# One decoder layer in single precision: squares of the head norms on ScalarE, and the pieces of h built in single steps

## The chip, the cores and the metric

One Trainium2 chip, one core of it. The time is the device time of one execution in microseconds; a kernel is given by the median of several runs. Inside the core TensorE (PE) does matrix products, with its weight loads beside them; VectorE (DVE), ScalarE (ACT) and GpSimd (POOL) do everything elementwise; SyncE and the queues of ACT start transfers between HBM and the on-chip memory. Each engine takes its own instructions in a fixed order and stands still when the next one has to wait.

## What is computed

```python
def decoder_layer(x, ...):                       # x: 1024 prompt rows and 8 x 4 sample rows, 1024 wide
    h = rmsnorm(x, ln1)
    proj = h @ w_in
    aq, ak, av, sh, sB, sC, dqkv, dz, da, db, gl = jnp.split(proj, split_at, axis=-1)
    oa = attn_fn(aq, ak, av, sinks)              # A) banded attention with sinks
    ob = sB * causal_dwconv(sC * sh)             # B) gated short convolution
    oc = gated_deltanet(dqkv, dz, da, db, ...)   # C) conv, SiLU, l2norm of q and k, delta rule, gated RMSNorm
    gates = jax.nn.sigmoid(gl)
    x = x + (gates[0] * (oa @ w_br_a) + gates[1] * (ob @ w_br_b) + gates[2] * (oc @ w_br_c)) @ w_o
    up = causal_dwconv(rmsnorm(x, ln2) @ ffn_up)
    return x + (jax.nn.silu(up[gate]) * up[val]) @ ffn_down
```

Everything is float32. The 1024 prompt rows and 32 sample rows are kept together as T = 1056 columns of transposed tiles [128, 1056]. The output is the normed result and the new caches and states.

## The kernel before

**Split products.** TensorE is fed with numbers in a reduced format (fp32r). `split(src, hi, lo, eng)` (L214-217) makes two of them out of a float32 tile: `hi` is a cast by ScalarE (L216), `lo = src - hi` is a subtraction on the engine named (L217). A product is the sum of three: high by high, high by low, low by high.

**Jobs.** `ORDER` (L158-163) is the list of projections by name: `d4 hbd q0 d5 d6 dpairs d7 D0 D2 ...` at the start, `... z0 z1 z2 hb b3 z3 less pairs g15 G16 G00 ...` in the middle. A plain job such as d5, q0 or z3 multiplies one 128-column block of `w_in` with all of h in three groups of 24 matmuls (`products`, L324), one per third of T. Each group writes to one of three PSUM banks that are used in turn (`mm`); the job's evacuation frees it: ScalarE at L1202 for q, k and z, VectorE at L721 for the d blocks. A capital letter is a pair of blocks, done by seven half-size products in place of eight (`Pairs.run`, L1428, in the order b11, t1, t2, b22, t3, b21, t4), with copies of intermediate results by ScalarE (L1437) and sums by VectorE (L1210, L1490). `Pairs.produce` (L1385 to L1391, then `split`) builds the seven weight pieces on VectorE and ScalarE for the D pairs (`dpp`) and on GpSimd and ScalarE for the G pairs (`gp`).

**Pieces of h.** The D pairs and the G pairs need, for each of four pairs of row blocks of h, the pieces t1 = b12 - b11, t2 = b22 - t1, t3 = b22 - b12, t4 = b21 - t2, each [128, 528] and each split. `h_build` makes them: for `dpp` out of `hT` while d4 to d6 run, and for `gp`, after adding high and low part again (L1811), while b3, z3 and g15 run. The subtractions are on VectorE (L1823), the low parts of t1 and t3 on GpSimd and those of t2 and t4 on VectorE (L217).

**Sums of squares.** After its convolution (L359) and SiLU (L705, L706) each of the eight q and k head blocks is stored to `raw_d` as it is; `norm_sums` then calls `sums`, which squares the tile in place (L604, so it has to wait for the store to have read it), splits the square and adds up its columns on TensorE (L612). `out_norm` calls `sums` for the four heads of the delta rule's output; `rsqrt_rows` copies those sums (L619), sends them through HBM, and takes the power -1/2 of them on GpSimd in three instructions (L635).

**What sets the order.** The side work is written as generators ("lanes"). After every few matmuls `Lanes.tick` lets one lane do its next step, by a planner's clock in which `bg.after(us)` holds a lane back; a scheduler then puts each engine's instructions in order by their place in the program and their priority (evacuations have a high one). The first pair job (D0, later G16) starts when `h_build` is done.

Of the kernel before, what the change touches and what calls it, by code (L numbers as in the profile page):

```python
# [8 lines left out]
AF = mybir.ActivationFunctionType  # L9
ALU = mybir.AluOpType  # L10
# [9 lines left out]
T = SEQ + NS  # L20
# [133 lines left out]
RAWGAP, SUMGAP = 5.0, 10.0  # L154
GAHEAD, GADD, GLO = 4, (), ()
DPAHEAD, DPADD, DPLO, DTICK = 3, (1, 2, 3, 4), (0,), 6
HGAP, HSTART = (0.0, 1.5), 12
KEPT = 4  # L158
ORDER = """
d4 hbd q0 d5 d6 dpairs d7 D0 D2 D8 D10 delta  # L160
# [12 lines left out]
def trunk(tc, A, O, cst_d):  # L173
    nc = tc.nc
    bg = Lanes()
# [33 lines left out]
    HT, HU = T // 2, T // 4  # L209
    mm = nc.tensor.matmul  # L210
    transpose = nc.tensor.transpose
    f32 = lambda ap: ap.bitcast(F32)

    def split(src, hi, lo, eng):  # L214

        nc.scalar.copy(hi, src)  # L216
        eng.tensor_tensor(lo, src, f32(hi), op=ALU.subtract)  # L217
# [122 lines left out]
    def group(tg):  # L340

        return slice(tg * TG, (tg + 1) * TG), (TG if tg < 2 else TG - NS), (0 if tg < 2 else NS)
# [257 lines left out]
    def sums(src, sa, r, acc, wait):  # L600


        (hi, ha), (lo, la) = grab([128, T], F32R), grab([128, T], F32R)
        nc.vector.tensor_tensor(src, src, src, op=ALU.mult)  # L604
        split(src, hi, lo, nc.vector)
        sa.drop()
        yield bg.after(wait)
        for tg in range(NTG):
            cc, q = group(tg)[0], 46 - 16 * tg - r
            for x in (hi, lo):  # L610
                acc[1] -= 1
                mm(acc[0][:48, :TG], hot[:, q:q + 48], x[:, cc], start=acc[1] + 1 == acc[2], stop=not acc[1])  # L612
        ha.drop()
        la.drop()
# [33 lines left out]
    def norm_sums(j, sil, sa):  # L648
        if not qk_acc:
            qk_acc["a"] = keep(1) + [8 * 2 * NTG] * 2  # L650
        dma(raw_d[j], sil)
        over = bg.after(RAWGAP)
        yield lambda: over() and room2(2)()
        yield from sums(sil, sa, 2 * j, qk_acc["a"], SUMGAP)
        if not qk_acc["a"][1]:
            held[0] -= 1
            bg.add(norm_lane())
# [468 lines left out]
    def out_norm():  # L1126
# [14 lines left out]
        for h in range(4):  # L1141
            if h < 3:
                yield sb.room(2)
                load_o(h + 1)
            yield sb.room(2)
            yield from sums(os[h], sb, 2 * h, acc, 4.5)
# [130 lines left out]
    def grab(shape, dt=F32):  # L1277
        return sb.take(shape, dt), sb

    def room2(n):  # L1280
        return lambda: sb.live + n <= sb.n
# [507 lines left out]
    gp = Pairs(8, [], GAHEAD, 6, GADD, GLO, 12)  # L1789
    hb = pieces(8)  # L1790

    def h_build(pp):

        def room(n):
            return lambda: room2(n if done.get("att", 0) > 2 * NB else n + 3)()

        if pp is gp:
            yield lambda: done.get("prep", 0) == NB and done.get("att", 0) >= HSTART
        else:
            room = room2  # L1800
        yield room(6)
        pp.scratch = [grab([128, SLOT]) for _ in range(3)]
        for p in range(4):
            yield room(4)
            t, _ = grab([128, T])
            if pp is dpp:
                vp, vq = hT[p], hT[p + 4]
            else:
                vp, vq = (x[0][:, :T] for x in pp.scratch[:2])
                for v, k, eng in zip((vp, vq), (p, p + 4), (nc.vector, nc.gpsimd)):  # L1810
                    eng.tensor_tensor(v, f32(hh[k]), f32(hl[k]), op=ALU.add)  # L1811
            b11, b12, b21, b22 = vp[:, :HT], vp[:, HT:T], vq[:, :HT], vq[:, HT:T]
            t1, t2 = t[:, :HT], t[:, HT:T]
            hb["b11"][p] = hh[p][:, :HT], hl[p][:, :HT], None
            hb["b21"][p] = hh[p + 4][:, :HT], hl[p + 4][:, :HT], None
            hb["b22"][p] = hh[p + 4][:, HT:T], hl[p + 4][:, HT:T], None

            def put(piece, src, eng):
                w = grab([128, T], F32R)
                hb[piece][p] = w[0][:, :HT], w[0][:, HT:T], w[1]  # L1820
                split(src, w[0][:, :HT], w[0][:, HT:T], eng)

            sub = lambda out, x, y: nc.vector.tensor_tensor(out, x, y, op=ALU.subtract)  # L1823
            over = bg.after(HGAP[pp is gp])
            yield over
            sub(t1, b12, b11)
            put("t1", t1, nc.gpsimd)
            yield room(1)
            sub(t2, b22, t1)
            put("t2", t2, nc.vector)  # L1830
            over = bg.after(HGAP[pp is gp])
            yield lambda: room(1)() and over()
            sub(b12, b22, b12)
            put("t3", b12, nc.gpsimd)
            yield room(1)
            sub(t1, b21, t2)
            put("t4", t1, nc.vector)
            sb.drop(3 if pp is dpp else 1)
            if pp is gp:
                over = bg.after(HGAP[1])  # L1840
                yield over
        hb["ready"] = True

    def pairs_start(pp):
# [59 lines left out]
    for b in range(3):  # L1904
# [3 lines left out]
        for m in range(0, 8, 2):  # L1908
            named[f"G{b}{m}"] = lambda b=b, m=m: pair_job(gp, C_GL + b * D + m * 128, lambda: gate_pair(b, m), last_gates)
    named["hb"] = lambda: step(lambda: bg.add(h_build(gp), False))  # L1910
    named["hbd"] = lambda: step(lambda: bg.add(h_build(dpp), False))
    named["dpairs"] = lambda: step(lambda: pairs_start(dpp))
    named["pairs"] = lambda: step(lambda: pairs_start(gp))
# [504 lines left out]
```

## Time and profile before

| | us |
|---|---|
| median of 3 runs | 1893.98 |
| lowest and highest run | 1889.29, 1896.81 |
| profiled execution, whole | 1890.09 |
| its span, first to last instruction | 1888.0 |
| TensorE, VectorE, GpSimd, ScalarE busy | 1781.3, 1127.3, 1061.4, 778.3 |
| mean granted TensorE clock | 0.968 |

The profile is of one execution. TensorE is busy for 94% of the span; the time that is left is some hundred microseconds, in a few places. The times of single instructions come from the same execution, which took 2.1 us more than its span and stood 3.9 us below the median of the runs.

### The profile page before, as it was taken

What the parts mean: (1) busy time and instruction counts of PE and PEld (TensorE: products, weight loads), DVE (VectorE), ACT (ScalarE), POOL (GpSimd) and SP (SyncE); (2) the same over time, 40 slices, a digit from 0 to 9 for tenths busy, and PEclk for the clock granted to TensorE, in tenths of its full rate; (3) what the DMA queues carried; (4) which work ended last, traced back from release to release, by engine and by line L of the source; (5) the groups of instructions that cost most, each with busy time, mean ns of one, the idle gap of its engine ahead of it and who ended that gap; (6) DMA issues with size and microseconds to landing.
All of it is one profiled execution on the core that took longest, in us unless ns stands there. A gap on an engine that the chain in (4) does not pass through costs nothing.

```text
span 1888.0 us, 33612 instructions
## 1 busy us (share of the span) xinstructions
PE 1781.3 (94%) x12862; PEld 1741.7 (92%) x12862; DVE 1127.3 (60%) x1944; ACT 778.3 (41%) x1626; POOL 1061.4 (56%) x985
## 2 busy tenths in 40 slices
PE   5899999898999997999999999999999999899997
PEld 3799988798999996999999999999999999899997
DVE  5578823354478779431234766777777787764324
ACT  5444522221245433444321345445545544454433
POOL 3345534334333329986447246988998988344542
PEclk8899999997999997999999999999999999999999
DMA  6312597656566533553464344444444442695513
GB/s 220 104 47 80 180 301 219 173 154 147 154 163 168 153 104 110 198 207 112 166 223 142 121 137 148 142 153 156 161 147 153 144 161 98 239 369 185 178 48 108
DMA packets 299633, 300.79 MB, mean 159 GB/s; under 512 B 56708, under 2 KB 231280, under 8 KB 299456
## 3 DMA queue, kind: packets, MB, share of 16 engines
q1 hardware_dynamic: 239984, 261.94, 43.3%
q10 hardware_dynamic: 59488, 36.70, 6.8%
q8 instruction: 101, 1.65, 0.4%
q14 instruction: 60, 0.49, 0.1%
HBM read 205.30 MB, written 95.28 MB: 159 GB/s over the span
## 4 chain that ended last, share of the span: by engine, by line
PE 50%; DVE 3%; DMA 2%; ACT 2%; POOL 2%; issue 1%; SPq 0%; DVEq 0%; ACTq 0%; POOLq 0%
PE mm L1428 16%; PE mm L324 12%; PE bgps L1428 12%; PE bgps L2294 2%; PE bgps L2296 2%; PE bgps L2295 2%; PE mm L2295 1%; PE mm L2296 1%; PE mm L2294 1%; DVE slot L2134 1%; DMA slot<-hb_d 1%; DMA wr<-in_ffn_up 1%; DVE slot L2176 1%; DMA st_d<-slot 0%; ACT slot L216 0%
## 5 line engine op out<-in xcount | busy, mean ns | idle before, releaser
L324 PE MATMUL mm<-slot,wh 128*128 128x352 f32 x2496 | 625.3, 331 | 19.6 <-ACT slot L1202 10.9
L324 PEld LDWEIGHTS mm<-slot,wh 128*128 128x128 f32 x2496 | 442.8, 192 | 27.0 <-ACT slot L1202 11.7
L324 PE MATMUL mm<-slot,wl 128*128 128x352 f32 x1248 | 409.7, 328 | 1.9 <-POOL wl L217 1.9
L217 POOL TENSOR_TENSOR wl<-wr,wh 128x1024 fp32r<-128x1024 f32 (+1 forms) x62 | 127.1, 2050 | 233.3 <-ACT wh L216 224.1
L324 PEld LDWEIGHTS mm<-slot,wl 128*128 128x128 f32 x1248 | 239.1, 192 | 4.0 <-POOL wl L217 2.2
L216 ACT CAST slot<-slot 128x528 fp32r<-128x528 f32 (+4 forms) x224 | 143.2, 660 | 129.7 <-DVE slot L1823 27.9
L217 POOL TENSOR_TENSOR slot<-slot 128x512 fp32r<-128x512 f32 (+4 forms) x101 | 148.6, 1478 | 84.6 <-ACT slot L216 77.9
L1428 PE MATMUL mm<-slot,wh 128*128 128x264 f32 x1248 | 172.7, 291 | 17.7 <-ACT slot L1437 8.6
L217 DVE TENSOR_TENSOR slot<-slot 128x528 fp32r<-128x528 f32 (+3 forms) x123 | 130.3, 1073 | 94.2 <-ACT slot L216 87.5
L217 POOL TENSOR_TENSOR wl<-slot,wl 128x512 fp32r<-128x512 f32 x104 | 145.8, 1402 | 71.6 <-ACT wl L216 63.7
L1428 PEld LDWEIGHTS mm<-slot,wh 128*128 128x128 f32 x1248 | 163.0, 194 | 20.8 <-ACT slot L1437 9.9
L217 POOL TENSOR_TENSOR wh<-slot,wh 128x512 fp32r<-128x512 f32 x91 | 122.3, 1343 | 90.6 <-ACT wh L216 74.5
L1428 PE MATMUL mm<-slot,wl 128*128 128x264 f32 x1176 | 155.3, 284 | 0.6 <-ACT slot L1437 0.6
L1428 PEld LDWEIGHTS mm<-slot,wl 128*128 128x128 f32 x1176 | 147.8, 188 | 1.3 <-ACT slot L1437 1.0
L216 ACT CAST wh<-wr 128x512 fp32r<-128x512 f32 (+1 forms) x94 | 75.2, 800 | 161.6 <-PE mm L324 124.1
L2134 DVE SCALAR_TENSOR_TENSOR bgps<-slot,bgps 128x358 f32<-128x358 f32 x240 | 127.3, 588 | 11.8 <-ACT bgps L2132 11.0
L1428 PE MATMUL mm<-slot 128*128 128x264 f32 x936 | 124.5, 284 | 0.7 <-DVE bgps L1456 0.5
L1428 PE MATMUL bgps<-slot,wl 128*128 128x264 f32 x912 | 121.5, 286 | 0.9 <-ACT slot L1437 0.9
L1428 PEld LDWEIGHTS mm<-slot 128*128 128x128 f32 x936 | 118.1, 188 | 1.2 <-DVE bgps L1456 0.7
L1428 PEld LDWEIGHTS bgps<-slot,wl 128*128 128x128 f32 x912 | 116.1, 190 | 1.7 <-ACT slot L1437 1.1
L1428 PE MATMUL bgps<-slot,wh 128*128 128x264 f32 x864 | 113.6, 284 | 1.0 <-ACT slot L1437 0.9
L1428 PEld LDWEIGHTS bgps<-slot,wh 128*128 128x128 f32 x864 | 108.5, 188 | 1.4 <-ACT slot L1437 1.1
(402 smaller groups left out, 3666.9 us busy)
## 6 DMA issues: line engine op xcount, KB each, us to landing
wr<-in_w_in SPq DMA_DIRECT2D x32, 512.0 KB
g_d<-slot SPq DMA_DIRECT2D x24, 528.0 KB
slot<-g_d SPq DMA_DIRECT2D x24, 528.0 KB
ht_d<-slot SPq DMA_DIRECT2D x44, 264.0 KB
slot<-ht_d SPq DMA_DIRECT2D x44, 264.0 KB
wr<-in_ffn_up ACTq DMA_DIRECT2D x22, 512.0 KB
slot<-in_ffn_down SPq DMA_DIRECT2D x22, 512.0 KB
slot<-in_ffn_up ACTq DMA_DIRECT2D x22, 512.0 KB
```

The lines of the kernel that those rows point to most:

```text
L216: nc.scalar.copy(hi, src)
L217: eng.tensor_tensor(lo, src, f32(hi), op=ALU.subtract)
L324: mm(ps[:, :TG], a[:, k, :], b[k][:, cc], start=n == 0, stop=n == last)
L1428: mm(ps, w[:, x + k, :], b[y][:, c0:c0 + HU], start=not n and piece not in NESTED, stop=n == last, skip_group_check=piece in NESTED)
L2134: nc.vector.scalar_tensor_tensor(ps, cb[:, a + i:b + i], w(i), ps, op0=ALU.mult, op1=ALU.add)
L2176: sub = lambda out, y, z: nc.vector.tensor_tensor(out, y, z, op=ALU.subtract)
L2294: mm(ps, hi, bh, start=start, stop=False, skip_group_check=True)
L2295: mm(ps, hi, bl, start=False, stop=False, skip_group_check=True)
L2296: mm(ps, lo, bh, start=False, stop=stop, skip_group_check=True)
```

## The change

```diff
--- before.py
+++ after.py
@@ -154,7 +154,7 @@
 RAWGAP, SUMGAP = 5.0, 10.0
 GAHEAD, GADD, GLO = 4, (), ()
 DPAHEAD, DPADD, DPLO, DTICK = 3, (1, 2, 3, 4), (0,), 6
-HGAP, HSTART = (0.0, 1.5), 12
+HGAP, HSTEP, HSTART = (0.0, 2.0), 1.0, 12
 KEPT = 4
 ORDER = """
 d4 hbd q0 d5 d6 dpairs d7 D0 D2 D8 D10 delta
@@ -601,7 +601,7 @@
 
 
         (hi, ha), (lo, la) = grab([128, T], F32R), grab([128, T], F32R)
-        nc.vector.tensor_tensor(src, src, src, op=ALU.mult)
+        nc.scalar.activation(src, src, AF.Square)
         split(src, hi, lo, nc.vector)
         sa.drop()
         yield bg.after(wait)
@@ -1818,27 +1818,25 @@
             def put(piece, src, eng):
                 w = grab([128, T], F32R)
                 hb[piece][p] = w[0][:, :HT], w[0][:, HT:T], w[1]
-                split(src, w[0][:, :HT], w[0][:, HT:T], eng)
+                yield bg.after(HSTEP)
+                nc.scalar.copy(w[0][:, :HT], src)
+                yield bg.after(HSTEP)
+                eng.tensor_tensor(w[0][:, HT:T], src, f32(w[0][:, :HT]), op=ALU.subtract)
 
             sub = lambda out, x, y: nc.vector.tensor_tensor(out, x, y, op=ALU.subtract)
-            over = bg.after(HGAP[pp is gp])
-            yield over
+            yield bg.after(HGAP[pp is gp])
             sub(t1, b12, b11)
-            put("t1", t1, nc.gpsimd)
+            yield from put("t1", t1, nc.gpsimd)
             yield room(1)
             sub(t2, b22, t1)
-            put("t2", t2, nc.vector)
-            over = bg.after(HGAP[pp is gp])
-            yield lambda: room(1)() and over()
+            yield from put("t2", t2, nc.vector)
+            yield room(1)
             sub(b12, b22, b12)
-            put("t3", b12, nc.gpsimd)
+            yield from put("t3", b12, nc.gpsimd)
             yield room(1)
             sub(t1, b21, t2)
-            put("t4", t1, nc.vector)
+            yield from put("t4", t1, nc.vector)
             sb.drop(3 if pp is dpp else 1)
-            if pp is gp:
-                over = bg.after(HGAP[1])
-                yield over
         hb["ready"] = True
 
     def pairs_start(pp):
```

`put` is now a generator: it waits one planner microsecond, lets ScalarE cast the piece, waits one more, and gives the subtraction of the low part out on its own (L1824 of the kernel after; the cast is L1822 and the pieces' own subtractions L1826 there). The planner's gap ahead of t1 of the G pieces is 2.0 in place of 1.5, those ahead of t3 and after t4 are gone. In `sums`, the square in place is an activation with the function Square on ScalarE. The number of table loads on ScalarE is 12 in both kernels. No instruction is added or lost otherwise; outside the stretches from 60 to 225 and from 690 to 790 us the engines' orders are the same but for a few rows that move by some places.

Three places show how the order moves. The first is ScalarE's order while d4's SiLU (L705), q0's evacuations (L1202 with an `mm` bank) and the exponents of the delta rule's decay (L576 to L579) meet the casts of the first h pieces (slot_882, 888, 894 before). Before:

```order
L577 ACT_TABLE_LOAD
L577 ACTIVATE slot_332<-slot_332,smallT_149 128x33
L216 CAST wh_1003<-wr_834 128x1024
L216 CAST slot_882<-slot_878 128x528
L705 ACT_TABLE_LOAD
L705 ACTIVATE slot_823<-slot_823 128x1024
L706 ACTIVATE slot_823<-slot_823 128x32
L216 CAST slot_888<-slot_878 128x528
L216 CAST slot_894<-slot_170 128x528
L1202 ACTIVATE slot_836<-mm_837 128x352
L1202 ACTIVATE slot_836<-mm_898 128x352
L1202 ACTIVATE slot_836<-mm_968 128x352
```

After:

```order
L1822 CAST slot_855<-slot_851 128x528
L1202 ACTIVATE slot_836<-mm_837 128x352
L579 ACT_TABLE_LOAD
L579 ACTIVATE slot_328<-slot_332 128x33
L383 COPY slot_328<-bgps_817 128x32
L1202 ACTIVATE slot_836<-mm_875 128x352
L576 ACT_TABLE_LOAD
L576 ACTIVATE slot_332<-slot_332 128x33
L577 ACT_TABLE_LOAD
L577 ACTIVATE slot_332<-slot_332,smallT_149 128x33
L216 CAST wh_955<-wr_834 128x1024
L1202 ACTIVATE slot_836<-mm_916 128x352
```

q0's three evacuations stood behind a weight cast, three casts of pieces and the SiLU with its table load; now they stand ahead of the SiLU, with a single cast of a piece (slot_855) ahead of the first of them, and table loads of the exponents between them.

The second place is ScalarE's order at z3 (L1202), the last plain z block ahead of the G pairs. Before, with the casts of the squares further down:

```order
L216 CAST slot_6968<-slot_6938 128x528
L216 CAST slot_6976<-slot_6938 128x528
L216 CAST wl_6958<-slot_6773 128x512
L216 CAST slot_6993<-slot_6771 128x528
L216 CAST slot_6999<-slot_6938 128x528
L1202 ACTIVATE slot_6961<-mm_6962 128x352
L1202 ACTIVATE slot_6961<-mm_7007 128x352
L216 CAST wh_7087<-slot_6773 128x512
L1202 ACTIVATE slot_6961<-mm_7044 128x352
L1437 COPY slot_6771<-mm_7104 128x264
```

After, where slot_6956 and slot_7023 are the tiles of the output norm's first two heads:

```order
L1822 CAST slot_6966<-slot_6913 128x528
L1202 ACTIVATE slot_6944<-mm_6945 128x352
L1822 CAST slot_6986<-slot_6771 128x528
L1822 CAST slot_7004<-slot_6913 128x528
L604 ACTIVATE slot_6956<-slot_6956 128x1056
L216 CAST slot_7032<-slot_6956 128x1056
L604 ACTIVATE slot_7023<-slot_7023 128x1056
L1202 ACTIVATE slot_6944<-mm_6979 128x352
L1822 CAST slot_7048<-slot_7027 128x528
L216 CAST slot_7065<-slot_7023 128x1056
L216 CAST wh_7136<-slot_6773 128x512
L1202 ACTIVATE slot_6944<-mm_7013 128x352
```

The first z3 evacuation is now three rows behind the last weight cast; two squares and one of their casts stand ahead of the second.

The third place is GpSimd's order around the power of the output norm's sums (L635) and the weights of the pair G00. Before:

```order
L1387 TENSOR_TENSOR slot_6773<-slot_6773,wr_7213 128x512
L217 TENSOR_TENSOR wh_7405<-slot_7096,wh_7405 128x512
L217 TENSOR_TENSOR wl_7439<-slot_7096,wl_7439 128x512
L635 TENSOR_TENSOR slot_7349<-slot_7349,smallT_149 128x16 x2
L635 TENSOR_TENSOR slot_7349<-slot_7349,smallT_149 128x1
L217 TENSOR_TENSOR wh_7474<-wr_7213,wh_7474 128x512
L217 TENSOR_TENSOR wl_7510<-slot_6773,wl_7510 128x512
```

After:

```order
L217 TENSOR_TENSOR wl_7251<-slot_7143,wl_7251 128x512
L1385 TENSOR_TENSOR slot_6773<-slot_7143,slot_7145 128x512
L217 TENSOR_TENSOR slot_7182<-wr_6935,slot_7182 128x512
L635 TENSOR_TENSOR slot_7124<-slot_7124,smallT_149 128x16 x2
L635 TENSOR_TENSOR slot_7124<-slot_7124,smallT_149 128x1
L1387 TENSOR_TENSOR slot_6773<-slot_6773,slot_7143 128x512
L217 TENSOR_TENSOR wh_7281<-slot_6773,wh_7281 128x512
L217 TENSOR_TENSOR wl_7317<-slot_6773,wl_7317 128x512
```

L635 stood behind the weight sum L1387 and two low parts; now it stands ahead of L1387 and of the low parts wh_7281 and wl_7317, which are among the first weights of G00 there.

## Rows read from the trace of the kernel before

**Rows 1.** Page, part 1: busy us of each engine, share of the span, instructions.

```profile
PE 1781.3 (94%) x12862; PEld 1741.7 (92%) x12862; DVE 1127.3 (60%) x1944; ACT 778.3 (41%) x1626; POOL 1061.4 (56%) x985
```

**Rows 2.** Busy time by stage (us, count), then granted TensorE clock, DMA share, GB/s.

```profile
70.00:140.00 70.00, 58.66 (x352) 56.43 (x351) 55.98 (x68) 37.18 (x58) 29.71 (x30) 0.90 0.19 61
...
140.00:225.00 85.00, 81.49 (x651) 79.41 (x650) 73.69 (x82) 45.11 (x80) 47.74 (x48) 1.00 0.32 98
...
690.00:770.00 80.00, 67.04 (x442) 64.69 (x441) 72.39 (x69) 32.27 (x58) 66.92 (x35) 0.87 0.31 103
```

**Rows 3.** Timeline, TensorE, d5 to D0: start, length, instruction [idle before <-releaser].

```profile
88.64 0.95 PE L324 MATMUL mm<-slot,wh 128*128 128x352 f32 x2 [8.09 <-ACT slot L1202]
...
93.98 0.48 PE L324 MATMUL mm<-slot,wh 128*128 128x352 f32 x2
...
94.46 0.48 PE L324 MATMUL mm<-slot,wh 128*128 128x352 f32 x2
...
107.26 0.79 PE L324 MATMUL mm<-slot,wh 128*128 128x352 f32 x2 [3.07 <-DVE slot L721]
...
110.78 0.54 PE L324 MATMUL mm<-slot,wh 128*128 128x352 f32 x2
...
133.08 3.07 PE L1428 MATMUL mm<-slot,wh 128*128 128x264 f32 x24
...
139.39 1.00 PE L612 MATMUL bgps<-slot,hot 128*48 128x352 f32 x5 [0.17 <-DVE slot L217]
```

**Rows 4.** Timeline, ScalarE, same stretch.

```profile
88.13 1.16 ACT L1202 ACTIVATE slot<-mm 128x352 f32<-128x352 f32 x3
...
117.69 0.21 ACT L706 ACTIVATE slot<-slot 128x32 f32<-128x32 f32 x1
```

**Rows 5.** The squares (L604, who waited for them) and another Square (L459): min/median/max ns.

```profile
L604 DVE TENSOR_TENSOR slot<-slot x12: 1242/1260/2339, 92.6 to 760.7; 128x1056 f32<-128x1056 f32 x12
...
  ACT slot L216: 16.1, 8
...
L459 ACT ACTIVATE slot<-slot x9: 1053/1057/1067, 5.2 to 20.6; 128x1024 f32<-128x1024 f32 x8, 32x1024 f32<-32x1024 f32 x1
```

**Rows 6.** Timeline, VectorE, both builds.

```profile
87.93 0.70 DVE L217 TENSOR_TENSOR slot<-slot 128x528 fp32r<-128x528 f32 x1
...
120.79 1.26 DVE L604 TENSOR_TENSOR slot<-slot 128x1056 f32<-128x1056 f32 x1 [3.39 <-DMA raw_d<-slot]
...
137.59 1.74 DVE L217 TENSOR_TENSOR slot<-slot 128x1056 fp32r<-128x1056 f32 x1 [0.54 <-ACT slot L216]
...
721.06 2.96 DVE L217 TENSOR_TENSOR slot<-slot 128x528 fp32r<-128x528 f32 x1
...
730.51 2.31 DVE L604 TENSOR_TENSOR slot<-slot 128x1056 f32<-128x1056 f32 x1
```

**Rows 7.** Timeline, TensorE, the pair G16 and the start of G00.

```profile
731.72 4.88 PE L1428 MATMUL mm<-slot,wh 128*128 128x264 f32 x24 [6.20 <-ACT slot L1202]
...
740.17 2.80 PE L1428 MATMUL mm<-slot,wh 128*128 128x264 f32 x10 [3.58 <-ACT slot L1437]
...
744.85 0.81 PE L1428 MATMUL mm<-slot,wh 128*128 128x264 f32 x2 [1.88 <-DVE slot L217]
...
746.95 3.01 PE L1428 MATMUL mm<-slot,wh 128*128 128x264 f32 x12 [1.29 <-ACT slot L1437]
...
769.44 3.08 PE L1428 MATMUL mm<-slot,wl 128*128 128x264 f32 x24
...
772.36 3.06 PE L1428 MATMUL bgps<-slot,wh 128*128 128x264 f32 x24
```

**Rows 8.** Timeline, VectorE and GpSimd: the output norm's sums come back, and power, and a weight's low part.

```profile
777.20 0.18 DVE L628 TENSOR_SCALAR slot<-slot 128x33 f32<-128x33 f32 x1 [8.50 <-DMA slot<-ssq_d]
...
774.14 1.29 POOL L217 TENSOR_TENSOR wl<-slot,wl 128x512 fp32r<-128x512 f32 x1
...
777.46 6.34 POOL L635 TENSOR_TENSOR slot<-slot,smallT 128x16 f32<-128x16 f32 x3 [2.03 <-DVE slot L628]
```

## The prediction

> **What bounds the kernel now.** I read the page's busy line first: TensorE works 1781.3 of 1888.0 us [rows 1], so the change can at best take back part of some 107 us in which it stands. The windows by stage then tell whether those lie where the change works: TensorE is busy 58.66 of 70 us while the first pieces of h are built, with a mean granted clock of 0.90, and 67.04 of 80 us while the second set is, with VectorE busy 72.39 of 80 there; between 140 and 225 us it lacks only 3.5 [rows 2]. So I look at TensorE's timeline in two places.
>
> At the first, d5 starts 8.09 us late at 88.64: its first group needs a PSUM bank that ScalarE has not emptied [rows 3], because q0's three evacuations run only at 88.13, behind casts and the SiLU with its table load [rows 4]. After that wait the clock is down: the 18 matmuls from 88.64 to 93.98 take 5.34 us, while a triple at full clock takes 0.48 (93.98 to 94.46), so 2.46 are lost. d6 then waits 3.07 for a bank that VectorE has to empty (L721), and its next 12 matmuls, 107.26 to 110.78, lose another 3.52 - 1.92 = 1.6 [rows 3]. Half the rate fits 1.2 in place of 2.4 GHz. Together 15.2 us.
>
> At the second, G16's pieces come late: 6.20, 3.58, 1.88 and 1.29 us of waiting, 12.95 in all [rows 7]. The first is again a bank behind ScalarE's queue (L1202), the third a low part on VectorE. Behind these the pair runs without a gap until G00 starts at 769.44.
>
> **The change, part by part.**
>
> *Squares.* Twelve squares leave VectorE, 1.26 us each as a median, up to 2.34 [rows 5], and come to ScalarE. Its own Square of 128x1024 takes 1.057 [rows 5]; for 1056 columns I take 1.09 (scaled by columns). The wait for the store moves with it. From the SiLU's end at 117.90 [rows 4] to the square's start at 120.79 [rows 6] are 2.9 us: the store's price. Before, VectorE stood in that wait with evacuations behind it; now ScalarE does, with casts and evacuations behind it. ScalarE's cast already waited for the square, 16.1 us over eight times [rows 5], 2.0 each: so most of that wait is there now, in another form.
>
> *Single steps.* They add nothing: the same casts, subtractions and low parts; what changes is what they stand ahead of.
>
> *First build.* ScalarE's order shows q0's evacuations ahead of the SiLU, with one cast ahead of the first. The 8.09 goes, and with it the clock loss of 2.46. With d5 earlier, and three low parts of 0.70 [rows 6] on VectorE moved from before d4's square to behind it, the 3.07 and 1.6 go in their present form. Against the 15.2 I replayed the new order by hand with the row durations. What becomes late next: d6's first bank, about 1.0 (VectorE's evacuation stands behind the low part of d4's square, which comes 2.9 + 1.09 + a cast after the SiLU); the transposition of the decay's rows, 1.5 (its exponents follow more casts); D0's first bank, 0.9 (the same behind a low part of 1.26 to 1.74 [rows 6]); D0's b21 weights, 2.5 (a cast behind the waiting square); and, last, the column sums of d5's square ahead of D2, 3.5. That last one is the row that decides: today the sums wait for a low part on VectorE that ends at 139.33 [rows 3, 6]; in my replay it is ready at about 138.7, for VectorE has 56 of 70 us of work there [rows 2] and loses only three squares of 1.26 from it. 15.2 - 9.4 = 5.8 us gained. The bounds: 0, if VectorE's chain ends no earlier and every microsecond is waited for again ahead of D2; 15.2, if nothing new is late. I take 5.8, nearer to the first, since the nearest row (139.39, waiting for VectorE) says that VectorE's chain is already the last to arrive.
>
> *From 140 to 225 us.* Five more squares leave VectorE. TensorE lacks only 3.5 us: a gain of 0 to 3, I take 1.0.
>
> *Second build.* z3's first bank loses its queue of casts, so the 6.20 goes. But VectorE is the bound: its last low part released TensorE at 744.85 [rows 7]. Ahead of it, one square (2.31 [rows 6]) goes, and the new VectorE order has four low parts of squares, [128, 1056], pulled ahead of it: at 1.26 to 2.34 each (the squares' own span of prices, the same tiles) it ends at 744.85 - 2.31 + 5.0 to 9.4 = 747.6 to 751.9. TensorE has by then done more: both halves of b11 and t1 and the 24 sums of the squares, 14 matmuls at 0.121 [rows 7] and 24 at 0.16 (a third of the triple in [rows 3]) = 5.5 us more than at that point today. Of the 24.59 us to G16's end, 1.29 were waiting; 17.8 are left, and G16 ends at 765.4 to 769.7 against 769.44: 0 to 4 earlier. Then GpSimd: the power takes 6.34 us, after a round trip of the sums of 8.5 [rows 8]. Today it comes at 777.46, when G00's first weights are made; in the new order it stands ahead of a weight sum and two low parts of 1.29 [rows 8]. With the sums ready at about 753 it starts at about 762, ends at 768.3, and G00's weights are ready at 772.2. TensorE would want them about 3 us after G16's end. So G00's second piece ends at 775.8 to 778 by my replay, against 772.36 + 2.90 = 775.3. I take a loss of 0.5, with -6 (GpSimd's power and weights harmless, VectorE's low parts short) to +5 (all low parts at 2.34, the power in the way) as bounds.
>
> *The trace and a rule.* The same low part of 528 columns took 0.70 with GpSimd idle and 2.96 with it at work, the square 1.26 and 2.31 [rows 6]. So a square taken from VectorE in the second build may be worth more than its own length, as GpSimd's work next to it shortens too.
>
> The Trainium skill (SBUF — State Buffer, Who interferes with whom) says that a VectorE instruction with two inputs in SBUF and a GpSimd instruction that reads SBUF hold each other up, and that PE and ACT "never wait on anyone"; the trace agrees for VectorE, with the pairs just given. By that rule alone the four squares would free the shared port for some 9 us of the second build and its loss of 0.5 would become a gain; that is the second rival below.
>
> **The sum.** 5.8 + 1.0 - 0.5 = 6.3 us less than the profiled execution's 1890.1: 1883.8. That execution stood 3.9 below the median, so the median becomes 1887.7, 0.33% below. The runs span 7.5 us, 0.4%: 0.5% (9.5 us) is about what a measurement can tell from no change, that is, outside 1884.5 to 1903.5.
>
> **Rivals.**
>
> *VectorE's relief counts in full.* The first build keeps 8 to 10 of its 15.2 because the low parts come 1.26 us earlier for each square gone; the second gains 3 to 6 because four low parts at 1.26 rather than 2.34 and GpSimd's at 1.29 let the weights arrive in time. For it: 0.70 against 2.96 [rows 6]. Against it: GpSimd stays busy in the second build (66.92 of 80 us [rows 2]) with other reads, and the squares' low parts with two inputs stay on VectorE. Time: 1894 - 9 - 1 - 5, about 1878.
>
> *ScalarE is held by the stores* (slower). Each of eight squares now keeps ScalarE for 2.9 us of store and 1.09 of square, and what stands behind it are evacuations and weight casts that TensorE needs. The extra against today's 2.0 us of waiting is 2.0 a square, 16 in all; it decides from the point on which the row behind a square frees a bank that TensorE wants within 4 us, which is so for d6 and D0 by my replay, and the gain of the first build is gone with it. Time: 1888 + 16 = 1904. Against it: ScalarE has 37.18 of 70 us of work in the first stretch [rows 2], and behind the later squares of the q and k heads the pairs have copies on two banks ahead.
>
> *Nothing changes.* The h pieces and the squares' low parts arrive when they do today since VectorE is the same length of work in between, and D0 and G16 end where they do: 1894, within 2. For it: [rows 3], 139.39. Against it: q0's bank is certain to come earlier.
>
> **How the numbers follow.** Forecast 0.50 (1881 to 1894 about 1888: 0.16 below 1884.5, 0.34 within); full relief 0.20 (faster); stores 0.15 (0.14 slower, 0.01 within); nothing 0.15 (0.12 within, 0.03 slower). Faster 0.36, same 0.47, slower 0.17. The range takes in the full relief almost wholly and reaches towards the stores' 1904 until a tenth is left out on either side: 1875 to 1901.
>
> **What would show it.** Right: d5 starts at about 81 with no wait and full clock; waits of 1 to 4 us at d6, D0 and ahead of D2, and D2 no more than some 6 us earlier; z3 without its 6.20 wait; G16 ending at 765 to 770 and G00 waiting for weights behind L635. Wrong: if ScalarE's timeline shows squares with 3 us of idle before them and TensorE waiting for L1202 or L1437 behind them, the stores decide; if D0 and D2 start 8 or more us earlier, VectorE's relief counted in full; if TensorE's waits for L217 around 745 shrink below 1 us, my price for the four low parts was too high.

## The result: slower by 0.7%, and the profile after

| | before | after |
|---|---|---|
| median, us | 1891.78 (4 runs) | 1906.62 (4 runs) |
| lowest and highest run, us | 1889.29, 1896.81 | 1905.95, 1906.88 |
| ratio, 95% interval | | 1.007 [1.0056, 1.0085] |
| span of the profiled execution, us | 1888.0 | 1904.8 |

The kernel became 14.8 us slower where 6 us faster was forecast. (A fourth run of the kernel before has moved its median from 1893.98 to 1891.78.) The time lies outside the range given. It is close to that of the rival "ScalarE is held by the stores", but the experiments refute that rival's mechanism.

The windows of the changed kernel by stage, with the columns of [rows 2] (busy us and count of TensorE, its weight loads, VectorE, ScalarE, GpSimd, then granted clock, DMA share and GB/s):

```profile
70.00:140.00 70.00, 60.83 (x359) 57.59 (x357) 49.50 (x62) 35.65 (x53) 31.27 (x28) 0.93 0.17 54
140.00:225.00 85.00, 77.99 (x599) 75.00 (x600) 63.79 (x70) 51.23 (x89) 41.90 (x49) 0.98 0.29 91
690.00:770.00 80.00, 69.03 (x456) 65.56 (x456) 63.82 (x80) 33.98 (x62) 43.75 (x24) 0.91 0.34 108
```

Up to 140 us TensorE does a little more than before, 60.83 against 58.66 us [rows 2]. From 140 to 225 it does 3.5 us less, though VectorE is relieved there by 10 us. So what VectorE is rid of in work does not reach TensorE there.

ScalarE's and then VectorE's timeline of the first build, changed kernel (start, length, instruction, idle before and its releaser):

```profile
76.11 0.46 ACT L1202 ACTIVATE slot<-mm 128x352 f32<-128x352 f32 x1
...
85.82 0.22 ACT L706 ACTIVATE slot<-slot 128x32 f32<-128x32 f32 x1
...
90.95 1.09 ACT L604 ACTIVATE slot<-slot 128x1056 f32<-128x1056 f32 x1 [4.91 <-DMA raw_d<-slot]
...
92.06 1.07 ACT L216 CAST slot<-slot 128x1056 fp32r<-128x1056 f32 x1
...
93.17 1.26 DVE L217 TENSOR_TENSOR slot<-slot 128x1056 fp32r<-128x1056 f32 x1 [10.47 <-ACT slot L216]
...
94.34 1.82 DVE L1826 TENSOR_TENSOR slot<-slot 128x528 f32<-128x528 f32 x1
...
96.09 0.94 DVE L721 COPY slot<-mm 128x352 f32<-128x352 f32 x2
...
96.96 4.65 DVE L1824 TENSOR_TENSOR slot<-slot 128x528 fp32r<-128x528 f32 x2
...
122.48 1.26 DVE L217 TENSOR_TENSOR slot<-slot 128x1056 fp32r<-128x1056 f32 x1 [5.14 <-ACT slot L216]
...
127.85 0.94 DVE L721 COPY slot<-mm 128x352 f32<-128x352 f32 x2
...
145.47 0.69 DVE L217 TENSOR_TENSOR wl<-wr,wl 128x512 fp32r<-128x512 f32 x1 [6.13 <-ACT wl L216]
```

q0's evacuation (L1202) now runs at 76.11, so the 8.09 of [rows 3] are gone, as forecast. But after d4's SiLU ends at 86.04 ScalarE waits 4.91 us for the store to `raw_d`, then squares and casts. VectorE, whose next instruction is the low part of that square, stands idle for 10.47 us. Queued behind it are the pieces of h (L1826, L1824), seven of which stood ahead of the square before, and two evacuations (L721, 96.09) that TensorE waits for. The same comes again at 122.48, after 5.14 us, with the evacuations at 127.85 behind it; the 6.13 at 145.47 is a wait for a weight's cast, which itself waited for TensorE to free the buffer.

TensorE's timeline from d6 to D2, changed kernel:

```profile
96.66 0.95 PE L324 MATMUL mm<-slot,wh 128*128 128x352 f32 x2 [1.18 <-DVE slot L721]
...
99.46 0.71 PE L324 MATMUL mm<-slot,wh 128*128 128x352 f32 x2
...
105.08 0.35 PE L594 MATMUL bgps<-ident,slot 128*99 128x128 f32 x1 [1.66 <-ACT slot L590]
...
128.42 1.91 PE L1428 MATMUL mm<-slot,wh 128*128 128x264 f32 x7 [3.31 <-DVE slot L721]
...
129.68 4.38 PE L1428 MATMUL mm<-slot,wh 128*128 128x264 f32 x19
...
133.86 3.19 PE L1428 MATMUL bgps<-slot,wl 128*128 128x264 f32 x24
...
137.80 0.76 PE L1428 MATMUL bgps<-slot,wl 128*128 128x264 f32 x4 [0.75 <-ACT wl L216]
...
140.51 4.22 PE L1428 MATMUL bgps<-slot,wl 128*128 128x264 f32 x20 [1.96 <-POOL wl L217]
...
145.49 0.51 PE L1428 MATMUL mm<-slot,wl 128*128 128x264 f32 x2 [0.75 <-ACT wl L216]
...
148.88 1.01 PE L612 MATMUL bgps<-slot,hot 128*48 128x352 f32 x5 [0.93 <-DVE slot L217]
...
161.07 1.72 PE L1428 MATMUL mm<-slot,wh 128*128 128x264 f32 x12 [0.95 <-DVE slot L1210]
...
162.64 3.06 PE L1428 MATMUL bgps<-slot,wh 128*128 128x264 f32 x23
```

D0 starts at 128.42, 4.7 us earlier than the 133.08 of [rows 3]. Then it gives that back and more. It waits for weights that ScalarE and GpSimd made late (0.75, 1.96, 0.75), for the sums (0.93) and a VectorE sum (0.95). The start's 3.31 and the 1.96 are each followed by slow matmuls: 19 in 4.18 us from 129.68 to 133.86, where [rows 7] have 0.121 each (2.3), and 20 in 4.22. The granted clock is 0.50 of full from 128.4 to 134.0, which is the lower level, and 0.72 on the mean from 140.0 to 146.0. D0's last piece ends at 162.64 where D2 began at 155.00 before; 12 matmuls of D2, 1.5 us, are done by then. So D0 costs the 4.7 that were won and 6.1 more.

Where TensorE waits for the first operands of the delta rule, view of the waits from 225 to 310 us (us in total, times, longest), before and after:

```profile
PE bgps L795 <- DMA slot<-qkv_d: 5.1, 1, 5.1
```

```profile
PE bgps L795 <- DMA slot<-qkv_d: 14.1, 1, 14.1
```

The operands come from the normed q and k heads, through HBM. VectorE's copy of the finished sums (L619) and its last scaling of a head (L683) show by how much that chain is late, 7.4 and 8.0 us, first before, then after:

```profile
207.07 0.51 DVE L619 COPY slot<-bgps 48x352 f32<-48x352 f32 x1
...
270.13 1.26 DVE L683 SCALAR_TENSOR_TENSOR slot<-slot 128x1056 f32<-128x1056 f32 x1 [7.75 <-DMA slot<-ssq_d]
```

```profile
214.48 0.51 DVE L619 COPY slot<-bgps 48x352 f32<-48x352 f32 x1
...
278.18 1.26 DVE L683 SCALAR_TENSOR_TENSOR slot<-slot 128x1056 f32<-128x1056 f32 x1 [11.53 <-DMA slot<-ssq_d]
```

TensorE takes the operands at 287.48 before and at 297.24 after, 9.8 us later. The lateness then grows to 17.1 us at 687.50. Of that growth 4.8 us come in one stretch, between the same two waits (for L1058 and for L1464) in both kernels. Busy time, granted clock and the rest, before and after:

```profile
441.26:630.49 189.23, 187.88 (x1207) 180.04 (x1207) 115.61 (x211) 69.81 (x174) 64.62 (x55) 0.93 0.62 154
...
453.48:647.54 194.06, 192.71 (x1215) 184.75 (x1215) 116.44 (x211) 69.99 (x174) 65.88 (x55) 0.91 0.59 150
```

TensorE stands for 1.35 us of it in both; what differs is the granted clock. The same stretch took 194.46 us at 0.91 in the trace of run 1 below, which is no slower than the kernel before, and 188.33 at 0.94 in that of run 5, which is. So no run ties these 4.8 us to the change.

At the second build the waits are these, on TensorE, GpSimd and ScalarE, changed kernel:

```profile
763.33 2.35 PE L1428 MATMUL mm<-slot,wh 128*128 128x264 f32 x9 [5.51 <-ACT slot L1437]
...
784.85 0.51 PE L1428 MATMUL mm<-slot,wl 128*128 128x264 f32 x2 [3.66 <-ACT wl L216]
...
776.58 6.34 POOL L635 TENSOR_TENSOR slot<-slot,smallT 128x16 f32<-128x16 f32 x3
...
782.88 1.26 POOL L1387 TENSOR_TENSOR slot<-slot 128x512 f32<-128x512 f32 x1
...
784.18 0.62 ACT L216 CAST wl<-slot 128x512 fp32r<-128x512 f32 x1 [1.40 <-POOL slot L1387]
```

The 6.20 at z3 [rows 7] is gone; a wait of 5.51 has come at L1437. And the chain foretold at G00 is there: the power takes GpSimd from 776.58, the weight sum L1387 follows at 782.88, ScalarE casts it at 784.18, TensorE starts at 784.85 after 3.66 us. In this pair of traces the old and the new waits balance. From a wait for L1464 ahead of the second build to the end, the two kernels take as long as each other, 1217.6 (from 670.39) and 1217.3 us:

```profile
670.39 0.73 PE L324 MATMUL mm<-slot,wh 128*128 128x352 f32 x2 [2.46 <-DVE slot L1464]
```

```profile
687.50 0.95 PE L324 MATMUL mm<-slot,wh 128*128 128x352 f32 x2 [2.46 <-DVE slot L1464]
```

### The profile page after: what moved, and what is told of

Same layout as the page of the kernel before. It is cut to its first block, busy times and chain, and to the rows that moved or that the text cites. A ratio compares the mean times of both kernels' runs of the same rounds, so it can differ in the third digit from the quotient of the medians.

```text
span 1904.8 us, 33620 instructions
## 1 busy us (share of the span) xinstructions
PE 1788.2 (94%) x12862; PEld 1745.0 (92%) x12862; DVE 1104.9 (58%) x1932; ACT 789.6 (41%) x1638; POOL 1048.4 (55%) x985
## 4 chain that ended last, share of the span: by engine, by line
PE 47%; DVE 3%; ACT 2%; POOL 2%; DMA 2%; issue 2%; SPq 0%; ACTq 0%; DVEq 0%; POOLq 0%
PE mm L1428 14%; PE mm L324 12%; PE bgps L1428 11%; PE bgps L2292 2%; PE bgps L2294 2%; PE bgps L2293 2%; PE mm L2293 1%; PE mm L2294 1%; PE mm L2292 1%; DVE slot L2132 1%; DMA wr<-in_ffn_up 1%; ACT slot L216 1%; DVE slot L2174 0%; POOL wl L217 0%; POOL slot L217 0%
## 5 line engine op out<-in xcount | busy, mean ns | idle before, releaser
L217 POOL TENSOR_TENSOR wl<-slot,wl 128x512 fp32r<-128x512 f32 x104 | 141.8, 1364 | 76.5 <-ACT wl L216 72.9
L217 DVE TENSOR_TENSOR slot<-slot 128x528 fp32r<-128x528 f32 (+3 forms) x107 | 106.2, 1008 | 108.5 <-ACT slot L216 102.2
L216 ACT CAST slot<-slot 128x528 fp32r<-128x528 f32 (+4 forms) x192 | 123.3, 665 | 91.0 <-POOL slot L1389 27.0
L217 POOL TENSOR_TENSOR slot<-slot 128x512 fp32r<-128x512 f32 (+3 forms) x85 | 120.5, 1423 | 69.0 <-ACT slot L216 62.3
```

## The experiments

Theory A: the single steps put the pieces of h behind the wait for the store in VectorE's order; that ScalarE makes the squares is harmless. Theory B, the rival that came nearest in time: ScalarE, held by the stores, makes the loss. Ratios are to the kernel before, run on the same chip.

**1. Squares on ScalarE alone.**

```diff
# kernel before
-        nc.vector.tensor_tensor(src, src, src, op=ALU.mult)
+        nc.scalar.activation(src, src, AF.Square)
```

> h's pieces as in the kernel before; only the twelve squares go to ScalarE. Theory A (the single steps put the pieces of h behind the wait for the store in VectorE's order, the squares are harmless): 1888 to 1894, as before, and VectorE stands idle ahead of the first square's low part for less than 4 us, not 10.5. Theory B (ScalarE held by the stores makes the loss): 1902 to 1908, with TensorE waiting 14 us for the delta rule's operands as in the changed kernel.

Measured: 1887.97 us, ratio 0.9985 [0.9973, 0.9998]. VectorE's wait ahead of the first low part, and TensorE's old wait at d5:

```profile
97.68 1.26 DVE L217 TENSOR_TENSOR slot<-slot 128x1056 fp32r<-128x1056 f32 x1 [3.12 <-ACT slot L216]
...
91.42 0.96 PE L324 MATMUL mm<-slot,wh 128*128 128x352 f32 x2 [8.07 <-ACT slot L1202]
```

3.12 us in place of 10.47: the pieces are worked on while the store runs. The time lies at the lower edge of what theory A expected (1888 to 1894). The waits for stores on ScalarE cost nothing that the times show. That refutes theory B for this order of work, in which q0's evacuations still stand behind the SiLU; run 2 tests it in the order of the change.

**2. Single steps alone.**

```diff
# changed kernel
-        nc.scalar.activation(src, src, AF.Square)
+        nc.vector.tensor_tensor(src, src, src, op=ALU.mult)
```

> The pieces of h in single steps; the squares stay on VectorE. Theory A: 1901 to 1908, about the changed kernel's 1906.6, and VectorE idle for 5 us or more ahead of the first square with pieces of h behind it. Theory B: 1888 to 1894, as before.

Measured: 1905.22 us, ratio 1.0082 [1.0062, 1.0102]: the whole loss, with no square on ScalarE. VectorE's first square, and the line's waits for stores in all (us, times):

```profile
91.06 1.26 DVE L604 TENSOR_TENSOR slot<-slot 128x1056 f32<-128x1056 f32 x1 [8.28 <-DMA raw_d<-slot]
...
  DMA raw_d<-slot: 14.4, 4
```

The same line's waits in the kernel before:

```profile
  DMA raw_d<-slot: 9.6, 5
```

The 9.6 us over five have become 14.4 over four, and the pieces of h now stand behind them. The loss is there without a single square on ScalarE, so theory B is out in this order too. Which engine squares does not matter here; which work stands behind the wait does.

**3. The second build alone.** The first build and the squares of the q and k heads are as in the kernel before.

```diff
# changed kernel
-        nc.scalar.activation(src, src, AF.Square)
+        if wait == SUMGAP:            # q and k heads
+            nc.vector.tensor_tensor(src, src, src, op=ALU.mult)
+        else:
+            nc.scalar.activation(src, src, AF.Square)
...
+                if pp is gp:
                     yield bg.after(HSTEP)   # both pauses
```

> Single steps for the second build alone, squares on ScalarE for the output norm alone; the first build and the squares of the q and k heads as in the kernel before. Both theories: what is left is the second build's own share; by the traces of before and after, -1 to +1 us, so 1890 to 1893. If it is 5 us or more faster or slower, the account by traces is wrong.

Measured: 1893.72 us, ratio 1.002 [1.001, 1.0029], slower by some 2 to 5 us, a little more than the expected 1890 to 1893, which came from the account by traces. TensorE's two large waits and GpSimd's power (L638 here):

```profile
749.30 2.35 PE L1431 MATMUL mm<-slot,wh 128*128 128x264 f32 x9 [5.51 <-ACT slot L1440]
...
771.09 0.52 PE L1431 MATMUL mm<-slot,wl 128*128 128x264 f32 x2 [3.69 <-ACT wl L216]
...
762.83 6.33 POOL L638 TENSOR_TENSOR slot<-slot,smallT 128x16 f32<-128x16 f32 x3
```

They are those of the changed kernel (5.51 and 3.66 there).

**4. Squares of the q and k heads into a tile of their own.** None of these squares then waits for the store. Up to the first square VectorE's order stays that of the change, with the same four pieces of h ahead of it; further on many rows of VectorE, ScalarE and GpSimd stand in other places.

```diff
# changed kernel
+        sq, qa = grab([128, T])       # q and k heads only
-        nc.scalar.activation(src, src, AF.Square)
-        split(src, hi, lo, nc.vector)
+        nc.scalar.activation(sq, src, AF.Square)
+        split(sq, hi, lo, nc.vector)
...
-        yield lambda: over() and room2(2)()
+        yield lambda: over() and room2(3)()
```

> The changed kernel, but the eight squares of the q and k heads are written to a tile of their own, so that nothing waits for the store. Theory A: VectorE's idle stretch ahead of the first square's low part (10.5 us) shrinks by the store's 4.9 us and the later ones by some 3 each, D0's waits shrink with them; 1895 to 1902. Theory B: the whole loss goes, 1886 to 1892.

Measured: 1891.71 us, ratio 1.0015 [1.0002, 1.0027]. VectorE ahead of the first low part, and TensorE at D0's first piece and the sums in it:

```profile
87.58 1.26 DVE L217 TENSOR_TENSOR slot<-slot 128x1056 fp32r<-128x1056 f32 x1 [5.60 <-ACT slot L216]
...
125.40 1.73 PE L1434 MATMUL mm<-slot,wh 128*128 128x264 f32 x12 [0.91 <-DVE slot L727]
...
132.90 0.36 PE L618 MATMUL bgps<-slot,hot 128*48 128x352 f32 x1 [2.86 <-ACT slot L216]
```

VectorE's wait falls from 10.47 to 5.60, by the store's 4.9. Nearly the whole loss goes. That is the time theory B had given for this run (1886 to 1892); theory A had expected only half the gain (1895 to 1902) and missed. Since runs 1 and 2 speak against B, I read it as a correction of A: the steps' order is dear only together with the wait for the store, and that wait only together with the order. (As in the change, four subtractions and three low parts of the pieces stand behind d5's square here, but VectorE waits 2.53 us for it in place of 5.14.) How much of the gain comes from the rows that moved further on was not tested apart.

**5. The first build alone**, the complement of run 3.

```diff
# changed kernel; h_build for gp and the output norm's squares as before
+                if pp is dpp:
                     yield bg.after(HSTEP)   # both pauses
```

> The complement of the second-build run: single steps for the first build alone, squares of the q and k heads on ScalarE, the second build and the output norm's squares as in the kernel before. If the two builds' shares add up: the changed kernel's 1906.6 less the 3.8 of the second build, 1900 to 1905. Rival (the loss needs both builds): below 1896.

Measured: 1900.24 us, ratio 1.0048 [1.003, 1.0066]. This is within the sum of shares that was expected (1900 to 1905). VectorE's first wait is close to the 10.47 of the changed kernel, and D0 waits for its weights:

```profile
92.73 1.26 DVE L217 TENSOR_TENSOR slot<-slot 128x1056 fp32r<-128x1056 f32 x1 [10.74 <-ACT slot L216]
...
140.24 4.06 PE L1431 MATMUL bgps<-slot,wl 128*128 128x264 f32 x20 [2.99 <-POOL wl L217]
```

By the medians the first build costs about 9 us, the second about 4: 13 of the changed kernel's 14.8, so the shares add within their intervals. The second share is not in the changed kernel's own trace (1217.3 against 1217.6 us from L1464 on); in run 3's the same stretch takes 1220.9.

**6. The first build without the planner's pauses.** `HSTEP` is 0 in run 5's kernel.

```diff
# first-build kernel
-HGAP, HSTEP, HSTART = (0.0, 1.5), 1.0, 12
+HGAP, HSTEP, HSTART = (0.0, 1.5), 0.0, 12
```

> As the first-build run, with the planner's pauses of 1.0 us inside a step set to 0, so that the pieces are still single steps but fewer of them stand behind the first wait for a store (the last low part of a piece comes ahead of d5's convolution rather than behind d6's). Theory A (the loss is what is queued behind the wait on VectorE): between the two kernels, 1891 to 1899. Rival (splitting a piece into steps is enough): 1900 to 1905.

Measured: 1891.49 us, ratio 1.0006 [0.9996, 1.0017]. At the lower edge of theory A's 1891 to 1899. VectorE ahead of the first low part and at the copy of the sums, and TensorE at the b21 weights and at the operands of the delta rule:

```profile
92.08 1.26 DVE L217 TENSOR_TENSOR slot<-slot 128x1056 fp32r<-128x1056 f32 x1 [10.69 <-ACT slot L216]
...
208.90 0.51 DVE L622 COPY slot<-bgps 48x352 f32<-48x352 f32 x1
...
138.91 2.69 PE L1431 MATMUL bgps<-slot,wl 128*128 128x264 f32 x20 [0.60 <-POOL wl L217]
...
288.38 1.97 PE L798 MATMUL bgps<-slot 128*128 128x256 f32 x8 [2.45 <-DMA slot<-qkv_d]
```

VectorE stands idle just as long, 10.69 us, and 12 of the 16 subtractions of the pieces still come after it, as in run 5. Yet the loss is gone. So the first idle stretch is not the price, not even with these pieces behind it. What differs is the second wait, that for d5's square. In the changed kernel and in runs 2 and 5 four subtractions and three low parts of the pieces stand behind it on VectorE, ahead of or between D0's weights; in run 6 none do, as in the kernel before and in run 1. The pieces are done ahead of d5's convolution, D0's weights are not pushed behind them, and TensorE waits 0.60 for them where it waited 2.99 in run 5. This is not the whole difference: D0 even starts later than in run 5 (130.86 against 128.12). But the sums are done at 208.90 where run 5 has 214.11, and the delta rule's operands are there at 288.38 in place of 295.91.

**7. Own tile and the first build's steps.** Run 4's squares, with `h_build` for gp as in the kernel before.

```diff
# own-tile kernel
+                if pp is dpp:
                     yield bg.after(HSTEP)   # both pauses
...
-HGAP, HSTEP, HSTART = (0.0, 2.0), 1.0, 12
+HGAP, HSTEP, HSTART = (0.0, 1.5), 1.0, 12
```

> Single steps in the first build, q and k squares on ScalarE into a tile of their own, the second build as in the kernel before, the output norm's squares on ScalarE. If the store's wait was what made the first build's steps dear and the second build's steps cost 3.8: the own-tile run's 1891.7 less 3.8, 1886 to 1889, below both kernels. Rival (the own-tile run gained by something else in the second build): 1890 to 1894.

Measured: 1888.61 us, ratio 0.9985 [0.9972, 0.9997], within the expectation. With the squares in a tile of their own the first build's steps are harmless at least; the second build's steps cost run 4 its 3 us.

**8. The second build with the power off GpSimd.**

```diff
# second-build kernel
-        if n == 8:
+        if n in (4, 8):               # square root and reciprocal, not the power
```

> The second-build run (1893.7), with the output norm's power -1/2 made by a square root on ScalarE and a reciprocal on VectorE, as for the q and k heads, so that its three instructions of 6.3 us leave GpSimd's queue. If their place ahead of G00's weights makes the wait of 3.7 us at G00: 1889 to 1891 and that wait below 1 us. Rival (the weights are late for another reason): 1893 to 1895, the wait stays.

Measured: 1885.86 us, ratio 0.9975 [0.9964, 0.9987]: 7.9 us below run 3 in the medians. At G00 TensorE's wait for the weight cast is gone; the largest one after G16's is now

```profile
773.43 1.84 PE L1431 MATMUL bgps<-slot 128*128 128x264 f32 x13 [1.30 <-ACT slot L1440]
```

The expectation was 1889 to 1891: the wait of 3.7 us at G00 came from the power on GpSimd, as expected, but the gain is larger than that wait. Where the rest came from these traces do not settle.

**9. Both repairs**: run 4's own tile and run 8's power.

```diff
# own-tile kernel
-        if n == 8:
+        if n in (4, 8):
```

> The changed kernel with both repairs: q and k squares to a tile of their own, and the output norm's power by a square root on ScalarE and a reciprocal on VectorE. If the two repairs add: the own-tile run's 1891.7 less the 7.9 that the power's move gave, 1882 to 1886, the fastest so far. Rival (the power's move gains only where G16 starts at that moment): 1888 to 1892.

Measured: 1884.07 us, ratio 0.997 [0.996, 0.998]. This is within the expectation, and the lowest median of all; the interval overlaps that of run 8.

**10. The kernel before with the power off GpSimd.**

```diff
# kernel before
-        if n == 8:
+        if n in (4, 8):
```

> The kernel before with only the output norm's power moved off GpSimd. There it stood behind G00's first weights and nothing at G00 waited for it: 1888 to 1893, no change. Rival (the power's 6.3 us on GpSimd cost time in any order): 1882 to 1887.

Measured: 1895.45 us, ratio 1.0024 [1.0012, 1.0036]: neither expectation; a little slower, by 2 to 7 us. In the order of before, taking the power off GpSimd gains nothing. The edit also gives ScalarE two more table loads of 1.28 us; whether they make the loss was not tested.

**11. Squares on ScalarE and the power off GpSimd**, pieces of h as before.

```diff
# squares-only kernel of run 1
-        if n == 8:
+        if n in (4, 8):
```

> Squares on ScalarE, pieces of h as in the kernel before, the power moved off GpSimd. If the power costs nothing in the order of before: 1886 to 1890, as the squares-only run. Rival: 1880 to 1885.

Measured: 1887.05 us, ratio 0.9978 [0.9965, 0.9991], as without the power's move (run 1) within the intervals. So in these runs the power matters only in the order that the steps of the second build make.

## Why the prediction was wrong, step by step

*Right.* q0's evacuations moved forward, and the 8.09 and the clock loss behind it went. The waits that were foretold are all there: d6's bank, the transposition, D0's bank, the weights of b21, the sums in D0. So is the power ahead of G00's weights, and G16's first 6.20 is gone.

*The first step that failed: the first build's sum.* I held 9.4 us of new waits against 15.2 freed. Up to D0's start the three waits put at 3.4 came to 1.18 + 1.66 + 3.31 = 6.2, and the matmuls behind the first ran at half rate, which the sum did not have (9 of them in 2.80 us, 96.66 to 99.46, against 1.44). D0 began 4.7 us earlier instead of 11.8. These two explain 4.1 us of the difference. Of the other 3, 1.3 stood in the changed trace before its first piece of h (a copy on ScalarE, L383, is at 73.51 in place of 72.25), and two waits for sums took 0.8; the rest is not assigned. Inside D0, 6.0 us were forecast (2.5 and 3.5); it lost 10.8. Its waits came to 5.3, and the two slow stretches took another 3.7. So the term was 6.1 us of loss where 5.8 of gain stood. The mechanism was seen, in parts; its size was set too small. One cause is the price of the store: 2.9 us, taken from d5's square alone, where d4's took 4.91 (and 5.4 before, from the SiLU's end at 87.17 to the square at 92.57). The other is that the sum was set as if the pieces of h still filled the waits for the stores, while the orders already showed them behind. Run 4 takes the wait for the store away, run 6 the pieces behind the second wait (d5's square), and in both the loss is gone.

*The second: a term that the sum lacks.* It has none for the stretch from 225 to 690 us, which the change does not touch, so it stood there at 0. The changed trace is 6.6 us late at the end of D10 (226.0 to 232.6, by the end of the pair's last matmul) and 17 late at a wait for VectorE's L1464 that both have (630.49 to 647.54). A late D0 makes the sums late, these the normed heads, these the delta rule's operands, for which TensorE waits 14.1 in place of 5.1. I followed the squares to TensorE's sums and no further. The traces, one of each kernel, show where this path decides (us from the start):

| kernel | end of D10 | sums copied | operands there | median of the runs |
|---|---|---|---|---|
| before | 226.0 | 207.1 | 287.5 | 1891.8 |
| changed | 232.6 | 214.5 | 297.2 | 1906.6 |
| run 1 | 230.2 | 208.7 | 287.9 | 1888.0 |
| run 2 | 233.6 | 214.6 | 296.1 | 1905.2 |
| run 4 | 225.8 | 198.9 | 285.5 | 1891.7 |
| run 5 | 232.3 | 214.1 | 295.9 | 1900.2 |
| run 6 | 230.2 | 208.9 | 288.4 | 1891.5 |

The three kernels with the first build's loss have their operands 8 to 10 us late, and no other has. A late end of D10 alone does not tell: runs 1 and 6 end D10 4 us late and lose nothing. How long TensorE waits for the operands does not tell either (2.4 to 14.1 us), since that depends on what else it still has to do. Of the 17 us at L1464, 4.8 came later, at a lower granted clock, and cannot be put down to the change.

*From 140 to 225 us*, 1.0 was to be gained; from D2 to the end of D10 0.5 more was lost. Small.

*The second build*: a loss of 0.5, between a gain of 6 and a loss of 5, was given; alone it measured 3.8. The power ahead of the weights was seen, and run 8 confirms it. What the sum did not have was the wait that took the place of z3's: 5.51 at L1437. In its readings, the 0.70 of a low part "with GpSimd idle" is not quite that: a subtraction on GpSimd starts at 88.30, within it. The one at 81.27 ran with GpSimd idle and took 0.69, so the comparison with 2.96 holds.

*The rivals.* "ScalarE is held by the stores" gave 1904 and lies next to the time. That is luck. Half of its sign came: the first squares on ScalarE have 4.91 and 2.80 us of idle time before them. But in the first build TensorE then waits for VectorE's L721, and not for L1202 or L1437. Runs 1 and 2 refute it: with all twelve squares on ScalarE there is no loss, and with none there the whole loss is. "VectorE's relief counts in full" (the first rival in the list; the prediction's remark on the shared port calls it the second) has run 1 for it in a small way, 2.8 us by the ratio with the order of work left alone.

## What to carry to other kernels

When work is cut into smaller steps, look at what each long wait on that in-order engine now has behind it: the steps that used to fill the wait may stand behind it, and the wait that was free then sets the time. Here it was not the longest wait that told (10.7 us in run 6, with no loss) but the one with work behind it that the next product's weights had to follow. The order tells that before the kernel runs; follow it to the end of the chain, through a round trip over HBM if there is one. A wait made only by overwriting a tile that a transfer still reads goes away with a tile of its own; here the new order then cost little or nothing (runs 4 and 7).

## What the runs showed of the hardware

ScalarE's square of [128, 1056] took 1.07 to 1.09 us in run 1, as scaled from the row of 1024 columns; VectorE's took 1.24 to 3.46 us in run 2. In the changed kernel, TensorE's wait of 3.31 us at D0's start was followed by a granted clock of 0.50 (128.4 to 134.0), the lower of its two levels. After the wait of 1.18 at d6, with a shorter one (0.32) just before it, 9 matmuls took 2.80 us in place of 1.44. After the one of 1.66 at the transposition the granted clock was 1.00 (105.0 to 110.0). So the length of one wait alone does not tell whether the clock falls.
